# The last three sums of a seven-product pair split as one piece of 1536 columns

## The chip, the cores and the metric

The kernel runs on one core of one Trainium2 chip. The metric is the device time of one execution in microseconds; three runs of the kernel before gave 1866.25, 1866.78 and 1867.99 us, median 1866.78 us.

## The reference

One layer for 256 tokens of width 2048: a gated feed-forward block, a mixer, a second feed-forward block, each with an RMS norm ahead and a residual sum behind, and a last norm.

```python
x = x + 0.5 * swiglu(rmsnorm(x, ffn1_norm), w_gate, w_up, w_down)   # D_FF = 5632
h = rmsnorm(x, mix_norm); proj = h @ w_in                            # q, k, v of two mixers, gates, indexer
# retention over chunks of 128 tokens, sparse attention with the 64 best keys per query, rope on q and k
x = x + concat([ro, ao]) @ w_out
x = x + 0.5 * swiglu(rmsnorm(x, ffn2_norm), w_gate2, w_up2, w_down2)
return rmsnorm(x, final_norm)
```

Everything is in float32. Most of the arithmetic is in the six large products of the feed-forward blocks.

## The kernel before

**Precision.** A weight of 32 bits is split into two numbers of the matmul's format: `hi`, a rounded copy that ScalarE makes, and `lo = raw - hi`, that VectorE makes. A product of blocks is three matmuls (left hi by hi, left hi by lo, left lo by hi). So each weight that arrives by DMA passes once through ScalarE and once through VectorE before TensorE can use it.

**Pairs.** The wide products (gate and up, down, output) go by `wide` (L179). Two 128-row slices of the weights with 1024 columns, a pair, are one load of 128 x 2048 elements in a tile `raw` (ring of three). A pair of kind "C" takes the eight plain block products, 24 matmuls of 512 columns, from two pieces of 1024 columns. A pair of kind "S" is one step of a scheme with seven products, 21 matmuls, and needs sums of weight blocks: VectorE forms four of them in place (`less`, L278), three in piece 1 and one in piece 2. A pair of seven has four pieces: columns 512 to 1536, 1024 to 2048, 0 to 1024, and 1536 to 2048 alone.

**Chunks.** A chunk is 512 columns of gate and 512 of up with all eight pairs of K. The first chunk of each feed-forward block is plain; the other ten take the pairs in `ORDER` (L30): S C S C S C C C. A block runs six chunks, then `down` for these (two halves d = 0, 1 of 12 pairs, four of them S), then five chunks, then `down` (two halves of 10 pairs, four S). In all there are 95 S pairs: 60 in chunks, 32 in the down halves, 3 in the output product.

**Order.** The order on every engine is the program's own (`manual_schedule`). The main loop (L1089) walks the pieces: at step i it first runs `run_step(i)`, all work that was hung on that step, then `split(i + 4)`, then the matmuls of piece i. So a piece is split four pieces ahead, and `hi` and `lo` are rings of five tiles (`BUFS`, L39): the split of a piece waits until TensorE has finished the piece five before it. Work hung on steps: `sums_of` (L479) after the last S pair of a chunk, `ups` (L542) one piece before a chunk's end, `hidden` (L550) at its end (silu on ScalarE, products on VectorE), transposes of the result into M1 and M6 (`turn`, L563) and their split (`left_pair`, L332) in the next chunk.

**Other places.** `tables` (L650) computes sine and cosine tables on VectorE in steps, from the start of the first down stretch; `yield n` lets n pieces pass. Ahead of the input projection `turn_early` (L592) transposes four column pairs of x into the banks M1, M5, M6, M7, and `turn_late` the other four; `split_x` (L300) reads each bank by turns with ScalarE and VectorE. `rstd` and `row_of` (L439) make the row of norm factors by a small matmul of `diag`. The projection's chunks accumulate in bank pairs (`pair`, L93), the first in M5 and M6, the second in M1 and M7. `ret_mix` (L993) normalises and splits the retention's heads; the fourth call uses bank M8. In the plain first chunk, x itself is prepared pair by pair as it arrives (`first_x`, L397); for the three pairs that later chunks take as S, also the sums of its blocks (`s_of_x`, L362), in the order `FIRST` (L32).

Of the kernel before, what the change touches and what calls it, by code (L numbers as in the profile page):

```python
# [28 lines left out]
UP = "CSCSCSCC"  # L29
ORDER = (1, 0, 3, 2, 5, 4, 6, 7)  # L30
PLAIN = "CCCCCCCC"
FIRST = (0, 2, 4, 6, 7, 1, 3, 5)  # L32
DOWN = ("SCSCSCSCCCCC", "SCSCSCSCCC")
NH = 8
NI = 16
# [16 lines left out]
def layer(ctx: ExitStack, tc: tile.TileContext, a: dict, out: bass.AP):  # L52
# [103 lines left out]
    def mm_rows(chunk, n, kts, rhs, first, last):  # L156
# [21 lines left out]

    def wide(src, plan, left, x0=False, tail=False, order=None, sums=SUM):  # L179

        start = len(pieces)
        seen, last = {}, {}
        ending = [[], []]
        s_end = None

        def mm(i, off, a, m, at=None, p=None):

            for n, (u, v) in enumerate(((0, 0), (0, 1), (1, 0))):
                st = m not in seen
                seen[m] = 1  # L190
                e = [i, off, (pieces[i]["pair"], a), m, u, v, st, False]
                last[m] = e
                pieces[i if at is None else at]["mms"].append(e)

        for at, p in enumerate(order or range(len(plan))):
            kind = plan[p]
            loads.append([(0, block(src, 2 * at, 2 * at + 2, 1024))])
            if x0:
                loads[-1] = [lambda p=p: load_xT(p)] + [(o, loads[-1][0][1][:, o:o + n]) for o, n in
                                                        ([(0, 512), (512, 512), (1024, 1024)] if at == 0 else [(0, 2048)])]  # L200
            i = len(pieces)
            if kind == "C":
                tiles = [(0, 1024), (1024, 1024)]
                if x0 and at == 0:
                    tiles = [(0, 512), (512, 512), (1024, 1024)]
            else:
                tiles = [(512, 1024), (1024, 1024), (0, 1024), (1536, 512)]
            for k, (off, n) in enumerate(tiles):
                pieces.append(dict(load=len(loads) - 1, off=off, n=n, mms=[], left=left, pair=p,
                                   sums=k if kind == "S" else None, x=[p] if x0 and k == 0 else []))  # L210
            if kind == "C":
                for c in (1, 0):
                    for k in range(2):
                        off = 1024 * (1 - c) + 512 * k
                        j = max(j for j, (o, n) in enumerate(tiles) if o <= off)
                        for t in range(2):
                            if tail and p >= len(plan) - 2:
                                ending[t].append((i + j, off - tiles[j][0], p, (t, k), sums[f"{t + 1}{c + 1}"]))
                                continue
                            mm(i + j, off - tiles[j][0], (t, k), sums[f"{t + 1}{c + 1}"])  # L220
            else:
                for k, off, a, m in S_BLOCKS:
                    mm(i + k, off, a, m)
                s_end = len(pieces)

        ending[1].sort(key=lambda e: e[4], reverse=True)
        for t in range(2):
            for i, off, p, a, m in ending[t]:
                mm(i, off, a, m, i if t == 0 else len(pieces) - 1)
        for e in last.values():  # L230
            e[7] = True
        return start, s_end, len(pieces) - 1, len(pieces)
# [35 lines left out]
    def split(i):  # L268
        p = pieces[i]
        while n_loaded[0] < min(len(loads), p["load"] + 3):  # L270
            load(n_loaded[0])
            n_loaded[0] += 1
        for c in p.get("x", []):
            first_x(c, xT.pop(c))
        r = raws[p["load"]]
        raw = r[:, p["off"]:p["off"] + p["n"]]

        def less(a, b, o):  # L278
            V.tensor_tensor(r[:, o:o + 512], r[:, a:a + 512], r[:, b:b + 512], op=OP.subtract)  # L279


        k = p.get("sums")
        if k == 1:
            less(0, 1024, 1024)
        hi = new(wts, [P, 1024], F32R, "hi", BUFS)
        lo = new(wts, [P, 1024], F32R, "lo", BUFS)
        S.activation(hi[:, :p["n"]], raw, AF.Copy)  # L287
        if k == 1:
            less(0, 512, 0)
            less(512, 1024, 512)  # L290
        elif k == 2:
            less(1536, 512, 1536)
        V.tensor_tensor(lo[:, :p["n"]], raw, hi[:, :p["n"]].bitcast(F32), op=OP.subtract)  # L293
        split_of[i] = (hi, lo)

# [143 lines left out]
    def row_of(tok):  # L439

        diag = new(tmp, [P, 2, P], F32, "diag", 1)
        for t in range(2):
            V.tensor_scalar(diag[:, t], ident, tok[:, t:t + 1], None, op0=OP.mult)
        ps = small()
        yield 2
        for t in range(2):
            TE.matmul(ps[:, t * P:(t + 1) * P], lhsT=ones, rhs=diag[:, t], start=True, stop=True)
        return ps[:, :T]
# [142 lines left out]

    def turn_early(s_end, norm):  # L592

        for i, m in enumerate(("M1", "M5", "M6", "M7")):
            after(s_end + 2 + i, lambda i=i, m=m: turn_x(i, norm, m))

    def turn_late(end, norm, banks, later=0):

# [48 lines left out]

    rot_dram = new(dram, [P, 4, T], F32, "rot_dram")

    def tables():  # L650
        for k in range(2):
            ang, n = half_k("b"), half_k("sq")
            pi, pf = n[:, 0].bitcast(I32), n[:, 1]
            G.dma_start(pi, bass.AP(tensor=a["pos"].tensor, offset=a["pos"].offset, ap=[[0, P], [1, T]]))
            yield 4
            V.tensor_copy(pf, pi)
            for j in range(2):
                V.tensor_scalar(ang[:, j], pf, inv[:, k:k + 1], None, op0=OP.mult)
            yield 2
            V.tensor_scalar(n, ang, 1.0 / C_TWO_PI, None, op0=OP.mult)  # L660
            V.tensor_scalar(n[:, 0], n[:, 0], 0.25, None, op0=OP.add)
            yield 2
            V.tensor_scalar(n, n, MAGIC, None, op0=OP.add)
            V.tensor_scalar(n, n, MAGIC, None, op0=OP.subtract)
            for c in (C1, C2, C3):
                yield 2
                V.scalar_tensor_tensor(ang, n, -c, ang, op0=OP.mult, op1=OP.add)
            yield 1
            V.tensor_scalar(ang[:, 0], ang[:, 0], math.pi / 2, None, op0=OP.add)
            yield 1  # L670

            V.tensor_scalar(n, ang, 1.0 / C_TWO_PI, MAGIC, op0=OP.mult, op1=OP.add)
            V.tensor_scalar(n, n, MAGIC, None, op0=OP.subtract)
            for c in (C1, C2, C3):
                yield 2
                V.scalar_tensor_tensor(ang, n, -c, ang, op0=OP.mult, op1=OP.add)
            yield 2
            V.tensor_scalar(ang, ang, PI_DOWN, -PI_DOWN, op0=OP.min, op1=OP.max)
            yield 2
            S.activation(ang, ang, AF.Sin)  # L680
            yield 2
            V.tensor_scalar(ang[:, 1], ang[:, 1], sgn[:, k:k + 1], None, op0=OP.mult)
            G.dma_start(rot_dram[:, 2 * k:2 * k + 2], ang)
        yield 1
        act_table(AF.Silu)

# [14 lines left out]

    after(FIRST_SQ, first_squares)
    end = ffn(1, 0, 1, False)
    after(marks[1, 0, "down"] + 1, tables)
    after(marks[1, 1, "down"] + 4, load_tables)


# [6 lines left out]
        yield 2  # L714
        V.tensor_tensor(rot[:, :2], rot[:, :2], two(r_of[1]), op=OP.mult)

    after(m0 + 3, scaled_tables)

    heads = {}
    done_at = {}  # L720
# [26 lines left out]
    def cols(name, src, nchunks, idx=False, first=False):  # L747
# [7 lines left out]
        for c in range(nchunks):  # L755
            chunk = chunks[c]
            end = ends_[c] if c in ends_ else stream(src[c], kts, 256, 8, 4, rhs_x, chunk, mm_cols, 2)

            def done(chunk=chunk, c=c):
                if c % 2 == 0:  # L760
                    heads[name].append(big(shape=(P, 4, T)))
                return rope(chunk, 2, heads[name][c // 2][:, 2 * (c % 2):2 * (c % 2) + 2], idx,
                            3 if len(heads) == 1 and c == 0 else 1)

            after(end, done)
        done_at[name] = len(pieces)
# [42 lines left out]
    for c in range(4):  # L809
        chunk = Chunk()  # L810
        end = stream(a["w_rg"][c], list(range(KT)), 256, 8, 4, rhs_x, chunk, mm_cols, 2)

        def rg_done(chunk=chunk, c=c):
            b, g = evac(chunk, 2)
            V.tensor_tensor(g, g, two(r_of[1]), op=OP.mult)
            yield 1
            s = half_k("s")
            S.activation(s, g, AF.Silu)
            gate[c] = s

        after(end, rg_done)
        rg_end.append(end)
# [213 lines left out]
    after(s + 6, ret_norm)  # L1036
    for n in range(2):
        after(s + 7 + n, lambda n=n: ret_scale(n))
    for c in range(4):
        after(max(rg_end[c] + 2, s + 10 + 2 * c), lambda c=c: ret_mix(c))  # L1040

    class MixIn:
# [129 lines left out]
```

## Time and profile before

| | us |
|---|---|
| median of three runs | 1866.78 |
| profiled execution | 1868.15 |
| its span, first to last instruction | 1866.3 |
| TensorE busy | 1836.9 |
| VectorE busy | 1646.2 |
| ScalarE busy | 1072.9 |

The profiled execution is 1.4 us (0.07%) above the median. Busy time is the union of an engine's instructions; a busy TensorE is not TensorE at its peak, as its matmuls overlap. The mean granted TensorE clock is 0.997 of full speed. Idle time in front of an instruction is put down to the instruction of another engine that came last among those it waited for.

### The profile page before, as it was taken

Reading aid. Unit: us, or ns where it says so; the run is one execution under the profiler, and the core shown is the slowest. Engines: PE = TensorE matmul, PEld = TensorE weight load, DVE = VectorE, ACT = ScalarE, POOL = GpSimd, SP = SyncE. Lnnn points to the kernel's source line nnn. Section 1 sums busy time; section 2 is a strip of 40 time slices with the busy share of each in tenths; the row PEclk is TensorE's granted clock in tenths of the full one; section 3 lists DMA queues with packets and bytes.
Section 4 is the critical chain, followed back from the end, with each engine's and each line's share of the span. In section 5 each row is a group of like instructions: output and inputs, shape, how many; then the busy total and the mean of one; then the engine's idle time right before and its main releaser. Section 6 shows DMA issues by size and latency. Waiting matters only on the chain.

```text
span 1866.3 us, 22800 instructions
## 1 busy us (share of the span) xinstructions
PE 1836.9 (98%) x8643; PEld 1523.8 (82%) x8643; DVE 1646.2 (88%) x2122; ACT 1072.9 (57%) x1353; POOL 6.9 (0%) x17
## 2 busy tenths in 40 slices
PE   9999999999999999999999999999999999999997
PEld 7788787888888887988888888888888888888886
DVE  6999999999999997689865886799999889999997
ACT  7655655545565555656554566556555455555564
POOL 0000000000000000000000000000000000000000
PEclk9999999999999999999999999999999999999999
DMA  8545555565554544545434464555555555555454
GB/s 316 203 181 183 203 203 191 180 229 198 205 206 183 212 181 173 184 159 210 179 137 172 145 225 150 207 185 191 210 207 183 202 203 198 186 188 212 186 190 170
DMA packets 52237, 360.51 MB, mean 193 GB/s; under 512 B 5984, under 2 KB 5984, under 8 KB 9632
## 3 DMA queue, kind: packets, MB, share of 16 engines
q1 hardware_dynamic: 50976, 355.62, 51.6%
q0 software_dynamic: 576, 1.84, 0.3%
q10 hardware_dynamic: 576, 1.60, 0.3%
q8 instruction: 67, 1.10, 0.2%
q14 instruction: 42, 0.34, 0.1%
HBM read 356.42 MB, written 2.62 MB: 192 GB/s over the span
## 4 chain that ended last, share of the span: by engine, by line
PE 80%; DVE 12%; ACT 4%; issue 2%; DMA 2%; SPq 0%; ACTq 0%; DVEq 0%
PE M L236 63%; PE M L150 8%; DVE lo L293 7%; PE M L152 4%; DVE raw L279 2%; ACT hi L287 2%; PE M L168 1%; PE M L169 1%; PE M L167 1%; PE M L567 1%; DMA raw<-in_wgu 1%; DMA e<-in_xT 1%; DVE x L474 1%; ACT sq L416 0%; DVE e L477 0%
## 5 line engine op out<-in xcount | busy, mean ns | idle before, releaser
L287 ACT ACTIVATE hi<-raw 128x1024 fp32r<-128x1024 f32 (+2 forms) x859 | 844.6, 1006 | 561.5 <-DVE raw L279 359.5
L293 DVE TENSOR_TENSOR lo<-raw,hi 128x1024 fp32r<-128x1024 f32 (+2 forms) x859 | 976.4, 1159 | 122.1 <-ACT hi L287 108.7
L236 PE MATMUL M<-hi,xg 128*128 128x512 f32 x2240 | 725.5, 390 | 1.7 <-ACT e L546 1.5
L236 PE MATMUL M<-hi,mid 128*128 128x512 f32 x1690 | 527.4, 391 | 1.9 <-DVE e L1001 1.6
L236 PEld LDWEIGHTS M<-hi,xg 128*128 128x128 f32 x2240 | 420.5, 188 | 89.2 <-ACT e L546 1.9
L236 PE MATMUL M<-lo,xg 128*128 128x512 f32 x1120 | 437.9, 391 | 5.7 <-DVE lo L293 5.6
L236 PEld LDWEIGHTS M<-hi,mid 128*128 128x128 f32 x1690 | 317.2, 188 | 70.2 <-DVE e L1001 2.0
L236 PE MATMUL M<-lo,mid 128*128 128x512 f32 x845 | 329.8, 390 | 1.0 <-DVE lo L293 0.8
L279 DVE TENSOR_TENSOR raw<-raw 128x512 f32<-128x512 f32 x380 | 262.9, 692 | 12.7
L236 PEld LDWEIGHTS M<-lo,xg 128*128 128x128 f32 x1120 | 210.3, 188 | 55.5 <-DVE lo L293 12.7
L150 PE MATMUL M<-xg,hi 128*128 128x512 f32 x688 | 245.6, 401 | 0.4 <-DVE xg L307 0.3
L236 PEld LDWEIGHTS M<-lo,mid 128*128 128x128 f32 x845 | 158.6, 188 | 36.5 <-DVE lo L293 4.3
L152 PE MATMUL M<-xg,lo 128*128 128x256 f32 x645 | 180.9, 280 | 0.0
L150 PEld LDWEIGHTS M<-xg,hi 128*128 128x128 f32 x688 | 128.7, 189 | 30.3 <-issue 1.3
L236 PE MATMUL M<-hi,ext 128*128 128x512 f32 x360 | 141.2, 392 | 1.5 <-ACT s L557 1.4
L152 PEld LDWEIGHTS M<-xg,lo 128*128 128x128 f32 x645 | 122.3, 190 | 0.8
L236 PEld LDWEIGHTS M<-hi,ext 128*128 128x128 f32 x360 | 67.5, 188 | 18.9 <-DVE s L477 3.6
L236 PE MATMUL M<-lo,ext 128*128 128x512 f32 x180 | 70.1, 389 | 0.0
L477 DVE TENSOR_TENSOR s<-s,M 128x512 f32<-128x512 f32 x98 | 65.6, 683 | 1.9 <-PE M L236 0.9
L557 ACT ACTIVATE s<-s,r_tok 128x512 f32<-128x512 f32 x40 | 27.0, 718 | 53.5 <-DVE s L477 53.5
L477 DVE TENSOR_TENSOR e<-s,M 128x512 f32<-128x512 f32 x58 | 39.7, 684 | 1.0
L742 ACT ACTIVATE b<-e 64x512 f32<-64x512 f32 (+2 forms) x46 | 28.1, 612 | 19.8 <-DVE e L728 19.3
(176 smaller groups left out, 933.2 us busy)
## 6 DMA issues: line engine op xcount, KB each, us to landing
raw<-in_wgu SPq DMA_DIRECT2D x175, 1024.0 KB, 4.8
raw<-in_wd SPq DMA_DIRECT2D x88, 1024.0 KB, 4.8
raw<-in_w_out SPq DMA_DIRECT2D x16, 1024.0 KB, 4.9
raw<-in_w_iq SPq DMA_DIRECT2D x8, 1024.0 KB, 4.8
raw<-in_w_aq SPq DMA_DIRECT2D x8, 1024.0 KB, 4.7
raw<-in_w_rk SPq DMA_DIRECT2D x8, 1024.0 KB, 4.8
raw<-in_w_rq SPq DMA_DIRECT2D x8, 1024.0 KB, 4.7
raw<-in_w_rv SPq DMA_DIRECT2D x8, 1024.0 KB, 4.9
```

The source lines that it names most:

```text
L150: TE.matmul(acc, lhsT=hi[:, c:c + P], rhs=r, start=st, stop=sp)
L152: TE.matmul(acc[:, T:], lhsT=lo[:, c:c + P], rhs=r[:, :T], start=False, stop=False)
L167: TE.matmul(o, lhsT=h, rhs=hi[:, i * n:(i + 1) * n], start=st, stop=False)
L168: TE.matmul(o, lhsT=h, rhs=lo[:, i * n:(i + 1) * n], start=False, stop=False)
L169: TE.matmul(o, lhsT=l, rhs=hi[:, i * n:(i + 1) * n], start=False, stop=sp)
L236: TE.matmul(bank[m], lhsT=p["left"](pair, a)[u], rhs=split_of[i][v][:, off:off + 512], start=st, stop=sp)
L279: V.tensor_tensor(r[:, o:o + 512], r[:, a:a + 512], r[:, b:b + 512], op=OP.subtract)
L287: S.activation(hi[:, :p["n"]], raw, AF.Copy)
L293: V.tensor_tensor(lo[:, :p["n"]], raw, hi[:, :p["n"]].bitcast(F32), op=OP.subtract)
L477: V.tensor_tensor(o, a, b, op=OP.add)
L557: S.activation(u[b], bank[SUM[b]] if plain else u[b], AF.Silu, scale=r_tok[norm][:, t:t + 1])
L742: S.activation(b[p0:p0 + w], q[p1:p1 + w], AF.Copy)
```

## The change

A pair of seven gets a third piece of 1536 columns, blocks 0 to 1024 and the last sum, which is now written to columns 1024 to 1536; the fourth piece splits nothing and uses the third's tiles. These tiles, `hi3` and `lo3`, are of 1536 columns and have one buffer each, outside the rings. VectorE's `less` for the last sum now comes ahead of both copies by ScalarE, and one `lo` of 1536 columns follows. The room comes from the scratch for dynamic DMA, now 4096 bytes. Beside that, work hung on steps is moved: the order `FIRST`, the steps of `tables` and the start of the second table, `turn_early` (one step later, M5 last), `scaled_tables` and the small matmul in `row_of` (one step later each), the first two `rope`s, and the last `ret_mix` (right behind its gate).

```diff
-FIRST = (0, 2, 4, 6, 7, 1, 3, 5)
+FIRST = (0, 2, 1, 4, 3, 6, 5, 7)
...
-        (3, 0, "A22", "M4"))
+        (3, 1024, "A22", "M4"))
...
-                tiles = [(512, 1024), (1024, 1024), (0, 1024), (1536, 512)]
+                tiles = [(512, 1024), (1024, 1024), (0, 1536), (0, 1536)]
...
         k = p.get("sums")
+        if k == 3:
+            split_of[i] = split_of[i - 1]
+            return
+        n, ring = (1536, "3") if k == 2 else (1024, "")
         if k == 1:
             less(0, 1024, 1024)
-        hi = new(wts, [P, 1024], F32R, "hi", BUFS)
-        lo = new(wts, [P, 1024], F32R, "lo", BUFS)
-        S.activation(hi[:, :p["n"]], raw, AF.Copy)
+        hi = new(wts, [P, n], F32R, "hi" + ring, 1 if ring else BUFS)
+        lo = new(wts, [P, n], F32R, "lo" + ring, 1 if ring else BUFS)
         if k == 1:
+            S.activation(hi, raw, AF.Copy)
             less(0, 512, 0)
             less(512, 1024, 512)
         elif k == 2:
-            less(1536, 512, 1536)
+            less(1536, 512, 1024)
+            for o in (0, 512):
+                S.activation(hi[:, 2 * o:2 * o + 1024 - o], raw[:, 2 * o:2 * o + 1024 - o], AF.Copy)
+        else:
+            S.activation(hi[:, :p["n"]], raw, AF.Copy)
         V.tensor_tensor(lo[:, :p["n"]], raw, hi[:, :p["n"]].bitcast(F32), op=OP.subtract)
...
-        yield 2
+        yield 3
         for t in range(2):
             TE.matmul(ps[:, t * P:(t + 1) * P], lhsT=ones, rhs=diag[:, t], start=True, stop=True)
...
-        for i, m in enumerate(("M1", "M5", "M6", "M7")):
-            after(s_end + 2 + i, lambda i=i, m=m: turn_x(i, norm, m))
+        for i, m in enumerate(("M1", "M6", "M7", "M5")):
+            after(s_end + 3 + i, lambda i=i, m=m: turn_x(i, norm, m))
...
-    def tables():
+    def tables(second):
...
+            if k == 0:
+                yield second - now[0]
...
-    after(marks[1, 0, "down"] + 1, tables)
+    after(marks[1, 0, "down"] + 1, lambda: tables(marks[1, 0, "down"] + 31))
...
-    after(m0 + 3, scaled_tables)
+    after(m0 + 4, scaled_tables)
...
-                            3 if len(heads) == 1 and c == 0 else 1)
+                            (5, 4)[c] if len(heads) == 1 and c < 2 else 1)
...
             gate[c] = s
+            if c == 3:
+                ret_mix(c)
...
-    for c in range(4):
+    for c in range(3):
         after(max(rg_end[c] + 2, s + 10 + 2 * c), lambda c=c: ret_mix(c))
...
-    nc = bacc.Bacc("TRN2", target_bir_lowering=False, num_devices=1)
+    nc = bacc.Bacc("TRN2", target_bir_lowering=False, num_devices=1, dynamic_dma_scratch_size=4096)
```

In `tables`, every yield of 4 becomes 3, every 2 between two of VectorE's instructions becomes 1, and instructions that stood together are parted by a yield of 1: 22 steps for a table in place of 28.

## Rows read from the trace of the kernel before

**Rows 1.** The page: busy time by engine; shares of the chain that ended last.
```profile
PE 1836.9 (98%) x8643; PEld 1523.8 (82%) x8643; DVE 1646.2 (88%) x2122; ACT 1072.9 (57%) x1353; POOL 6.9 (0%) x17
...
PE 80%; DVE 12%; ACT 4%; issue 2%; DMA 2%; SPq 0%; ACTq 0%; DVEq 0%
```

**Rows 2.** Windows of four chunks: stretch, length, busy by engine, clock, DMA, GB/s.
```profile
52.23:98.05 45.82, 43.00 (x193) 35.02 (x192) 43.28 (x52) 29.31 (x35) 0.00 (x0) 1.00 0.53 197
98.05:141.12 43.07, 42.73 (x193) 35.02 (x191) 41.34 (x52) 25.19 (x29) 0.00 (x0) 1.00 0.52 196
...
1195.26:1237.63 42.37, 42.37 (x192) 35.18 (x191) 39.25 (x47) 25.45 (x29) 0.00 (x0) 1.00 0.54 199
...
1577.95:1620.34 42.39, 42.39 (x193) 35.17 (x192) 40.07 (x49) 25.51 (x29) 0.00 (x0) 1.00 0.55 199
```

**Rows 3.** VectorE's groups in the chunk at 98.05: busy, mean ns, idle before.
```profile
L293 DVE TENSOR_TENSOR lo<-raw,hi 128x1024 fp32r<-128x1024 f32 x19 | 22.8, 1221 | 0.9 <-ACT hi L287 0.5
L279 DVE TENSOR_TENSOR raw<-raw 128x512 f32<-128x512 f32 x12 | 8.3, 692 | 0.4
```

**Rows 4.** VectorE's timeline, one wait in the same chunk: start, us, instruction, idle.
```profile
126.88 1.22 DVE L293 TENSOR_TENSOR lo<-raw,hi 128x1024 fp32r<-128x1024 f32 x1 [0.55 <-ACT hi L287]
```

**Rows 5.** VectorE's timeline over pieces 1 to 3 of one S pair.
```profile
105.82 2.14 DVE L279 TENSOR_TENSOR raw<-raw 128x512 f32<-128x512 f32 x3
107.88 1.22 DVE L293 TENSOR_TENSOR lo<-raw,hi 128x1024 fp32r<-128x1024 f32 x1
109.13 0.69 DVE L279 TENSOR_TENSOR raw<-raw 128x512 f32<-128x512 f32 x1
109.74 1.82 DVE L293 TENSOR_TENSOR lo<-raw,hi 128x1024 fp32r<-128x1024 f32 x2
```

**Rows 6.** ScalarE's timeline, the copy of the same pair's fourth piece.
```profile
109.94 2.53 ACT L287 ACTIVATE hi<-raw 128x512 fp32r<-128x512 f32 x3 [0.80 <-DVE raw L279]
```

**Rows 7.** Groups by shape, whole span, of the pieces of 512 columns.
```profile
L293 DVE TENSOR_TENSOR lo<-raw,hi 128x512 fp32r<-128x512 f32 x97 | 66.4, 685 | 2.8 <-ACT hi L287 2.8
...
L287 ACT ACTIVATE hi<-raw 128x512 fp32r<-128x512 f32 x97 | 61.4, 633 | 81.4 <-DVE raw L279 66.4 <-PE M L236 13.9 <-DMA raw<-in_wgu 1.2
```

**Rows 8.** Windows of four down halves; the first two hold the tables.
```profile
270.67:337.10 66.43, 64.28 (x285) 52.39 (x284) 62.86 (x83) 34.35 (x38) 1.08 (x2) 1.00 0.55 197
337.10:400.36 63.26, 63.17 (x278) 51.64 (x276) 60.40 (x79) 32.13 (x35) 0.55 (x1) 1.00 0.56 204
613.52:667.04 53.52, 53.20 (x238) 43.46 (x236) 51.16 (x60) 30.07 (x34) 0.00 (x0) 1.00 0.55 206
...
1410.44:1473.91 63.47, 63.47 (x286) 52.63 (x284) 56.80 (x65) 34.55 (x37) 0.00 (x0) 1.00 0.55 200
```

**Rows 9.** TensorE's waits: line, waited for, us in total, times, longest.
```profile
PE M L236 <- DVE lo L293: 6.4, 19, 0.7
PE M L447 <- DVE diag L443: 2.4, 1, 2.4
PE M L567 <- DVE s L477: 2.0, 1, 2.0
PE M L236 <- DVE e L1001: 1.6, 1, 1.6
PE M L236 <- ACT e L546: 1.5, 1, 1.5
...
PE M L236 <- ACT s L557: 1.4, 1, 1.4
```

**Rows 10.** Timelines of TensorE, VectorE, ScalarE: a bank of x transposed, one split.
```profile
713.32 0.66 PE L405 MATMUL M<-ident,x 128*128 128x128 f32 x4 [1.38 <-DVE e L477]
...
710.75 0.48 DVE L307 SCALAR_TENSOR_TENSOR xg<-M,gains,xg 128x256 fp32r<-128x256 f32 x1 [0.54 <-ACT xg L306]
...
710.24 0.47 ACT L306 ACTIVATE xg<-M,gains 128x256 fp32r<-128x256 f32 x1 [0.55 <-DVE xg L307]
```

**Rows 11.** Window behind the wait for `diag`, columns as in group 2.
```profile
742.10:745.60 3.50, 3.44 (x12) 3.06 (x13) 3.50 (x6) 2.05 (x3) 0.00 (x0) 0.52 0.28 87
```

More of the change, by code (lines that the diff above doesn't have):

```diff
@@ L654, in tables @@
             G.dma_start(pi, bass.AP(tensor=a["pos"].tensor, offset=a["pos"].offset, ap=[[0, P], [1, T]]))
-            yield 4
+            yield 3
             V.tensor_copy(pf, pi)
@@ L658, in tables @@
                 V.tensor_scalar(ang[:, j], pf, inv[:, k:k + 1], None, op0=OP.mult)
-            yield 2
+            yield 1
             V.tensor_scalar(n, ang, 1.0 / C_TWO_PI, None, op0=OP.mult)
+            yield 1
             V.tensor_scalar(n[:, 0], n[:, 0], 0.25, None, op0=OP.add)
-            yield 2
+            yield 1
             V.tensor_scalar(n, n, MAGIC, None, op0=OP.add)
+            yield 1
             V.tensor_scalar(n, n, MAGIC, None, op0=OP.subtract)
             for c in (C1, C2, C3):
-                yield 2
+                yield 1
                 V.scalar_tensor_tensor(ang, n, -c, ang, op0=OP.mult, op1=OP.add)
@@ L672, in tables @@
             V.tensor_scalar(n, ang, 1.0 / C_TWO_PI, MAGIC, op0=OP.mult, op1=OP.add)
+            yield 1
             V.tensor_scalar(n, n, MAGIC, None, op0=OP.subtract)
             for c in (C1, C2, C3):
-                yield 2
+                yield 1
                 V.scalar_tensor_tensor(ang, n, -c, ang, op0=OP.mult, op1=OP.add)
-            yield 2
+            yield 1
             V.tensor_scalar(ang, ang, PI_DOWN, -PI_DOWN, op0=OP.min, op1=OP.max)
@@ L1038, in layer @@
         after(s + 7 + n, lambda n=n: ret_scale(n))
-    for c in range(4):
+    assert rg_end[3] + 1 >= s + 16
+    for c in range(3):
         after(max(rg_end[c] + 2, s + 10 + 2 * c), lambda c=c: ret_mix(c))
```

## The prediction

> **What bounds the kernel now.** I read first the busy times and the chain that ended last: TensorE is busy 98% of the span and holds 80% of the chain, VectorE holds 12% [rows 1]. A share over the whole span hides stages, so next come the windows of single chunks [rows 2]. A chunk in which nothing makes TensorE wait lasts 42.4 us (the one at 1195.26, the one at 1577.95); inside these there is still some 0.3 us of small delays, so TensorE's own need is about 42.1 us. The chunk at 98.05 lasts 43.07 us, with VectorE busy for 41.34 of them. Fourteen of the twenty chunks that hold S pairs look like this one; the other six, the first behind each plain chunk and the first two behind each down stretch, are shorter or, at 52.23, longer. The reader is to see that VectorE is 96% busy in such a chunk, and that its idle 1.73 us are not spare: the groups [rows 3] put 0.9 of them ahead of `lo`, of which only some 0.6 are waits for a free ring slot (0.55 in one place, [rows 4]); 0.4 stand ahead of `less`, 34 ns each for the result of the instruction before; and the rest is VectorE waiting for a copy or a silu of ScalarE that its own last result released. So VectorE needs 41.4 + 1.1 = 42.5 us for a chunk that TensorE could do in 42.1. In these chunks VectorE is the bound, by a little. TensorE's waits say the same: 19 waits for `lo` [rows 9], about one per chunk, at the first C pair of the new chunk.
>
> **The merged piece.** Removed is one instruction per S pair: `lo` of 1024 and `lo` of 512 become one of 1536. The pair of them takes 1.82 us from first start to last end [rows 5], with 0.685 for the second [rows 7], so the 1024 columns occupy 1.14 us before the next may start, and the 512 about 0.61. 512 columns more cost 0.53, which leaves 0.08 us of fixed cost: that is what a merge saves, and 1536 columns should take 1.67 where the two took 1.75.
>
> [...]
>
> Added is a wait. Now `less` for the last sum ends, and VectorE goes straight on to `lo` of piece 2, whose copy is long made; meanwhile ScalarE copies the 512 new columns, and that copy is hidden behind the 1.14 us of `lo` [rows 5, 6]. After the change the one `lo` needs that copy too, and nothing stands between `less` and `lo` in VectorE's queue, since both are inside one `split`. `less` starts at 109.13, the copy at 109.94, and it takes 0.633 [rows 5 to 7], so it ends at 110.57; VectorE could have started at 109.74. The wait is 0.83 us, with the step back to VectorE about 0.85. Bounds: not below 0.63 (the copy alone), not above 1.5 (that and the copy of 1024 columns behind it in ScalarE's queue, were it late). Behind it in VectorE's queue stand all later splits and evacuations. Net per S pair: 0.85 - 0.08 = +0.77 us of VectorE's queue; three pairs in a chunk, +2.3.
>
> The tiles of their own give something back: fewer pieces turn in the ring, so the 0.6 us of waits for slots go (I count them all as gone). `hi3` with one buffer costs nothing: its next use comes six pieces later and its split four ahead, so it waits for the piece just finished, as the ring did.
>
> **A chunk after.** 41.4 + 2.3 + 1.1 = 44.8 us against 43.1: +1.7, VectorE-bound, TensorE waiting some 2.5 us per chunk. Ten chunks have no lead from a slack stretch: +17.0. After a plain chunk or a down stretch VectorE has about 2 us of lead; I let it absorb the first chunk (0), most of the second (+0.3 twice behind a down stretch, +0.5 twice behind a plain one), and a part of the third behind a down stretch (+1.1 twice): +3.8.
>
> **Down halves.** With four S pairs VectorE needs 3.1 us more per half. The long half at 1410.44 has 63.47 of length and 56.80 of VectorE [rows 8], so only the debt of the chunk before it shows at its start: +2.0; its second half 0. The short halves (53.52, VectorE 51.16) become VectorE-bound like a chunk: +1.7 each for d = 0, +0.6 each for d = 1, twice: +4.6. The two halves with the tables carry some 6.1 us more of VectorE (62.86 against 56.80), now packed into the first 23 steps, where S pairs stand and where VectorE has no slack left. At least the half cannot be shorter than VectorE's need, 62.86 + 3.1 + 1.5 of unavoidable idle = 67.4 (+1.0); at most all of the table and the debt show (+5.5); I take +3.5 and, for the second table by the same reckoning from 60.40, +2.5.
>
> **Moved steps.** `FIRST` spreads the x sums over the plain chunk. The waits for ScalarE's `e` and `s` (1.5 and 1.4, [rows 9]) go, and the chunk at 52.23 becomes like the one at 1195.26: 45.82 - 42.37 = -3.4. Later `turn_early` frees the wait for `e` L477, -1.4 [rows 10]. But M5, now transposed last, is transposed at the first step of the projection, and M5 is where that first step accumulates: TensorE must wait until `ready` (two products of 512 columns, 0.61 us each as worked out above) and then ScalarE and VectorE by turns, some 0.5 us each, four times, have read the bank, less 0.7 us of its own transposes [rows 10]: +2.5, bounds 0 and 4.3 (with a clock loss as below). [...] Sum -3.0. The last `ret_mix` moves ahead of the wait for `e` L1001: -1.6, against three S pairs in the output product: +1.7; together 0. The 4 KB scratch and its few transfers on POOL, busy 6.9 us in all [rows 1]: between 0 and 2 us, off TensorE's path; I take 0. The `rope` steps shift work within the projection, where no `rope` stands among TensorE's waits [rows 9]: between -0.5 and 1, I take 0.
>
> **Sum.** 17.0 + 3.8 + 2.0 + 4.6 + 6.0 - 3.4 - 3.0 + 0 = +27.0 on the profiled 1868.15, which is 1.4 above the median of the runs: 1895.2 there, 1894 as a median.
>
> **Rivals.** *The free slots decide.* If ScalarE's copy were hidden after all (wait under 0.25 us, the point at which the chunk falls below 43.1), VectorE's need would fall to about 42.3, and fourteen chunks gain 0.8: -11; with -3.4, -4.1 - 1.4, -1.6 and some 2 in the table halves it ends near 1844. For it: the ring's waits are in the trace [rows 4], and the merge does shorten VectorE's queue. Against it: the copy needs `less`, and `lo` needs the copy, in a queue that is served in order. Chance 0.12. *The clock falls too.* If the new waits, at fourteen places 1.7 us or more, each sent TensorE to the lower level as the 2.4 us at 742 did, each would cost up to 1.7 more: +24, 1918. Against it: the wait of 2.0 us for `s` [rows 9] left the clock of its stretch at 1.00 [rows 8], and a TensorE that waits for VectorE anyway loses little. Chance 0.05. *Both sides cancel:* gains at the moved steps as above, the wait half hidden, no table cost: 1867. Chance 0.04.
>
> **How the numbers follow.** The forecast has 0.79. Its own ends: ScalarE's answers overlap better (chunk 44.2), no table cost and no wait for M5 give 1879; the tables in full, a clock loss at M5 and all old idle kept give 1908. Drawn a little wider, 1874 to 1910, it leaves out the faster rival and most of the clock's. About 0.2%, 3.7 us, is what a measurement of this kernel can tell from no change: faster 0.12, same 0.04, slower 0.84.
>
> **What would show it.** In the changed trace `lo` of 1536 columns should stand about 95 times, 1.75 us each, with some 0.85 us idle before each, put down to `hi`: about 80 us in all. The steady chunks should last near 44.8 us with VectorE without other gaps, and TensorE's waits for `lo` should grow from 6.4 to over 30 us. The waits for `diag`, `e` L546 and `s` L557 should be gone, and a new one of some 2.5 us should stand at the first matmul of the projection. I am wrong if the idle time before the long `lo` is short, or if chunks stay at 43 us with it.

## The result, and the profile after

The changed kernel takes 1912.66 us (median of four runs, 1911.50 to 1914.03) against 1867.38 for the kernel before beside it: a ratio of 1.0241, 95% interval 1.0229 to 1.0254, or +45.3 us. It is slower, as forecast, by the mechanism that was forecast, but by 18 us more than the sum said, and 2.7 us above the upper end of the range, 1910. The profiled execution took 1913.43 us, its span 1911.6.

The page of the changed kernel, busy times and the chain that ended last:

```profile
PE 1847.1 (97%) x8643; PEld 1523.0 (80%) x8643; DVE 1633.0 (85%) x2027; ACT 1058.7 (55%) x1353; POOL 6.9 (0%) x17
...
PE 42%; DVE 37%; ACT 11%; DMA 5%; issue 4%; ACTq 0%; SPq 0%; DVEq 0%
```

VectorE does less work than before, 13 us and 95 instructions less [rows 1], and yet its share of the chain went from 12% to 37%: an engine's share of the chain can grow because it waits, and not only because it works.

VectorE's groups by shape, whole span (busy us, mean ns | idle before, put down to):

```profile
L301 DVE TENSOR_TENSOR lo<-raw,hi 128x1024 fp32r<-128x1024 f32 x661 | 786.4, 1220 | 114.1 <-ACT hi L300 108.6
...
L301 DVE TENSOR_TENSOR lo<-raw,hi 128x1536 fp32r<-128x1536 f32 x95 | 167.1, 1759 | 66.4 <-ACT hi L298 66.4
```

The long `lo` stands 95 times with 1.76 us each, and 66.4 / 95 = 0.70 us of idle before each, all put down to the copy. VectorE's timeline over one such piece, and ScalarE's line for the copy of its last 512 columns:

```profile
153.79 1.22 DVE L301 TENSOR_TENSOR lo<-raw,hi 128x1024 fp32r<-128x1024 f32 x1
155.05 0.69 DVE L279 TENSOR_TENSOR raw<-raw 128x512 f32<-128x512 f32 x1
156.44 2.89 DVE L301 TENSOR_TENSOR lo<-raw,hi 128x1536 fp32r<-128x1536 f32 x2 [0.70 <-ACT hi L298]
```

```profile
155.78 0.63 ACT L298 ACTIVATE hi<-raw 128x512 fp32r<-128x512 f32 x1 [0.72 <-DVE raw L279]
```

Read it as a round trip: `less` starts at 155.05, the copy can start at 155.78, and `lo` at 156.44, 1.39 us after `less`. Before, the next `lo` began 0.61 us after `less` [rows 5]. So 0.78 us per pair went into the trip, where the prediction had 0.85; less the 0.08 that the merge saves, 0.70 against 0.77.

Windows of the changed kernel: two chunks (the one behind the plain first chunk, a steady one), the two halves with the tables, a short half, the chunk behind the second block's plain one, a long half (stretch, length, busy by engine, clock, DMA share, GB/s):

```profile
52.59:97.20 44.61, 43.31 (x193) 34.95 (x191) 38.90 (x45) 27.57 (x33) 0.00 (x0) 1.00 0.51 189
...
142.48:187.63 45.15, 43.31 (x193) 34.94 (x192) 41.10 (x49) 24.77 (x29) 0.54 (x1) 1.00 0.52 189
278.05:348.70 70.65, 64.94 (x286) 52.15 (x284) 63.90 (x81) 36.22 (x40) 1.08 (x2) 1.00 0.53 187
348.70:414.91 66.21, 63.49 (x277) 51.57 (x276) 59.95 (x75) 32.01 (x35) 0.54 (x1) 1.00 0.53 195
634.15:689.53 55.38, 53.51 (x237) 43.39 (x236) 50.80 (x56) 29.27 (x33) 0.00 (x0) 1.00 0.54 199
...
1222.56:1264.94 42.38, 42.38 (x193) 35.18 (x191) 38.07 (x44) 24.43 (x29) 0.00 (x0) 1.00 0.51 195
1445.10:1509.61 64.51, 64.09 (x285) 52.47 (x284) 57.23 (x63) 35.54 (x39) 0.00 (x0) 1.00 0.53 197
```

The steady chunk went from 43.19 us (141.12 to 184.31 before; 43.07 for its neighbour in [rows 2]) to 45.15 us, although VectorE is busy a little less in it, 41.10 against 41.49 us; the chunk at 1222.56 has the same splits and loses nothing, because it starts with a lead. TensorE's waits (line, waited for, us in total, times, longest):

```profile
PE M L236 <- DVE e L485: 21.9, 16, 1.6
PE M L236 <- DVE lo L301: 18.5, 43, 1.9
PE M L150 <- DVE xg L315: 6.2, 1, 6.2
```

The 40 us of the first two lines are VectorE's lateness as TensorE meets it: 18.5 us at a split, and 21.9 at `e`, the evacuation of a bank that stands behind the long `lo` in VectorE's queue. The third line is the start of the projection. The waits for `diag` and for `e` L1001 of [rows 9] are gone. The prediction wanted over 30 us in the waits for `lo` alone; there are 18.5, and more than half of the lateness shows at `e`.

Stage by stage, from windows cut at the same matmuls in both traces:

| stage | forecast | measured |
|---|---|---|
| ten steady chunks | +17.0 | +20.2 (1.7 to 2.3 each) |
| chunks with a lead | +3.8 | +7.4 (2.2, 1.3, 1.9, 1.9; five others 0) |
| halves with the tables | +6.0 | +7.2 (4.2, 3.0) |
| other down halves, without the last of the first block | +6.0 | +6.2 |
| plain chunk and the one behind it | -3.4 | -0.9 (+0.3, -1.2) |
| last half of the first block, projection | -2.4 | +3.4 |
| first chunk of the output product | 0 | +1.4 |
| ahead of the first and behind the last matmul of the wide products | 0 | +0.4 |
| sum | +27.0 | +45.3 |

### The profile page after: what moved, and what is told of

It is laid out like the page before. It is cut to its first block, busy times and chain, and to the rows that moved or that the text cites. A ratio compares the mean times of both kernels' runs of the same rounds, so it can differ in the third digit from the quotient of the medians.

```text
span 1911.6 us, 22558 instructions
## 1 busy us (share of the span) xinstructions
PE 1847.1 (97%) x8643; PEld 1523.0 (80%) x8643; DVE 1633.0 (85%) x2027; ACT 1058.7 (55%) x1353; POOL 6.9 (0%) x17
## 4 chain that ended last, share of the span: by engine, by line
PE 42%; DVE 37%; ACT 11%; DMA 5%; issue 4%; ACTq 0%; SPq 0%; DVEq 0%
PE M L236 25%; DVE lo L301 20%; DVE raw L279 10%; PE M L150 8%; ACT hi L300 7%; DMA raw<-in_wgu 4%; PE M L152 4%; DVE e L485 2%; ACT hi L298 2%; DVE s L485 1%; DMA raw<-in_wd 1%; PE M L168 1%; PE M L169 1%; PE M L167 1%; DVE x L482 1%
## 5 line engine op out<-in xcount | busy, mean ns | idle before, releaser
L301 DVE TENSOR_TENSOR lo<-raw,hi 128x1024 fp32r<-128x1024 f32 (+2 forms) x764 | 955.3, 1283 | 182.5 <-ACT hi L300 110.6
L300 ACT ACTIVATE hi<-raw 128x1024 fp32r<-128x1024 f32 (+1 forms) x574 | 576.5, 1046 | 187.9 <-PE M L236 70.9
L292 ACT ACTIVATE hi<-raw 128x1024 fp32r<-128x1024 f32 x95 | 101.0, 1063 | 309.9 <-DVE raw L279 307.5
L150 PE MATMUL M<-xg,hi 128*128 128x512 f32 x688 | 246.5, 402 | 6.2 <-DVE xg L315 6.2
L298 ACT ACTIVATE hi<-raw 128x1024 fp32r<-128x1024 f32 (+1 forms) x190 | 161.0, 847 | 107.6 <-DVE raw L279 106.9
L152 PE MATMUL M<-xg,lo 128*128 128x256 f32 x645 | 181.5, 281 | 0.0
L150 PEld LDWEIGHTS M<-xg,hi 128*128 128x128 f32 x688 | 129.3, 189 | 36.0 <-DVE xg L315 6.4
L152 PEld LDWEIGHTS M<-xg,lo 128*128 128x128 f32 x645 | 122.9, 190 | 0.7
```

The lines of the kernel that those rows point to most:

```text
L150: TE.matmul(acc, lhsT=hi[:, c:c + P], rhs=r, start=st, stop=sp)
L152: TE.matmul(acc[:, T:], lhsT=lo[:, c:c + P], rhs=r[:, :T], start=False, stop=False)
L292: S.activation(hi, raw, AF.Copy)
L298: S.activation(hi[:, 2 * o:2 * o + 1024 - o], raw[:, 2 * o:2 * o + 1024 - o], AF.Copy)
```

## The experiments

All differ from the changed kernel or from the one before by a few lines; the kernel before ran beside each, at 1867.3 to 1867.6 us.

**The moved steps alone**, with the old split:

```diff
 # against the changed kernel: tiles of pieces, split() and hi/lo rings as before
-                tiles = [(512, 1024), (1024, 1024), (0, 1536), (0, 1536)]
+                tiles = [(512, 1024), (1024, 1024), (0, 1024), (1536, 512)]
```

> The changed kernel with the split of before (two pieces of 1024 and 512 columns in the rings of five); all moved steps and the small scratch stay. Theory (the copy of the last sum, laid bare, makes the loss): steady chunks are back at 43.1 us, so this kernel lies within 6 us of before: gains at the first S chunk (about -3), at diag (-4.1) and at the last ret_mix (-1.6), against the wait for M5 with its half clock (+8 as the changed kernel's trace shows, less 1.4), together near 1867. Rival (the moved steps make the loss): above 1895, and the split alone near before.

Measured: 1867.79 us, ratio 1.000 (0.9991 to 1.0010). TensorE's longest wait, and a window around the entry to the projection:

```profile
PE M L150 <- DVE xg L307: 5.6, 1, 5.6
```

```profile
717.00:731.00 14.00, 8.36 (x41) 7.00 (x40) 8.31 (x12) 4.72 (x8) 0.00 (x0) 0.88 0.41 150
```

The moved steps with the 4 KB scratch cost nothing together, and none of the 45 us. But this zero is a balance: the `diag` wait is gone, and a wait of 5.6 us at the projection, with the clock down behind it (0.88 over the window shown, 0.51 from 726.0 to 729.4 us), has come.

**The split alone**, all steps where they were:

```diff
 # against the kernel before: the new split (a part of it is shown), the tiles of pieces 3 and 4, the scratch
+        n, ring = (1536, "3") if k == 2 else (1024, "")
...
+            less(1536, 512, 1024)
+            for o in (0, 512):
+                S.activation(hi[:, 2 * o:2 * o + 1024 - o], raw[:, 2 * o:2 * o + 1024 - o], AF.Copy)
```

> The kernel before with the new split, its tiles and the small scratch alone; no step is moved. Theory: 95 waits of 0.70 us ahead of the lo of 1536 columns, steady chunks near 45.2 us, no wait for M5, the waits for diag and at the first S chunk still there: 1905 to 1914. Rival (moved steps): 1862 to 1872.

Measured: 1911.46 us, ratio 1.0233 (1.0218 to 1.0248), +43.8. A steady chunk, the window behind the wait for `diag`, and TensorE's waits:

```profile
145.04:190.16 45.12, 43.31 (x193) 34.95 (x191) 41.10 (x49) 24.77 (x29) 0.54 (x1) 1.00 0.52 190
...
764.00:772.00 8.00, 5.59 (x34) 4.78 (x33) 7.36 (x16) 5.60 (x9) 0.00 (x0) 1.00 0.40 132
```

```profile
PE M L236 <- DVE e L485: 21.8, 16, 1.7
PE M L236 <- DVE lo L301: 15.8, 42, 1.5
...
PE M L236 <- ACT e L554: 2.8, 1, 2.8
PE M L455 <- DVE diag L451: 2.4, 1, 2.4
```

The split carries all the loss: +43.8 and +0.2 from the run above leave 1.3 of the 45.3 us for the two together. The waits of 2.4 us for `diag` and of 2.8 us for `e` are as long as those of the kernel before or longer, and yet the clock was 1.00 in the window shown, and its mean over the traced execution was 0.998, where the kernel before had 0.997.

**Is it the wait, or the tiles?** The tiles, both copies and their order stay; only the long `lo` becomes two instructions, so that 1024 columns can go while the last 512 are copied:

```diff
-        V.tensor_tensor(lo[:, :p["n"]], raw, hi[:, :p["n"]].bitcast(F32), op=OP.subtract)
+        if k == 2:
+            for a, b in ((0, 1024), (1024, 1536)):
+                V.tensor_tensor(lo[:, a:b], raw[:, a:b], hi[:, a:b].bitcast(F32), op=OP.subtract)
+        else:
+            V.tensor_tensor(lo[:, :p["n"]], raw, hi[:, :p["n"]].bitcast(F32), op=OP.subtract)
```

> The changed kernel with one edit: lo of the 1536-column piece is made by two instructions, of 1024 and then 512 columns, in the same tiles. The copy of the last sum is then hidden behind the first of them. Theory: the idle time ahead of lo falls from 66 us in all to under 5, VectorE gains 95 times 0.62 (0.70 less 0.08 for one instruction more), steady chunks fall to 42.5 to 43.4, and the kernel to 1865 to 1877 (the wait for M5 stays). Rival (tiles with a single buffer hold ScalarE and VectorE back): the time stays above 1900.

Measured: 1867.83 us, ratio 1.0003 (0.9994 to 1.0012). VectorE's groups, and a steady chunk:

```profile
L303 DVE TENSOR_TENSOR lo<-raw,hi 128x1024 fp32r<-128x1024 f32 x95 | 115.8, 1219 | 0.0
...
L303 DVE TENSOR_TENSOR lo<-raw,hi 128x512 fp32r<-128x512 f32 x95 | 65.1, 685 | 0.0
```

```profile
527.09:570.19 43.10, 42.93 (x192) 35.04 (x191) 41.19 (x52) 24.89 (x29) 0.00 (x0) 1.00 0.51 195
```

The idle time goes from 66.4 us to 0.0 and the whole loss with it, with two tiles, scratch and moved steps in place. A wait of 0.70 us, 95 times, in a queue where everything behind it waits too, was the loss. The tiles of their own give nothing back: 43.10 us is the old chunk.

**The size of the wait.** The two copies change places, so that ScalarE makes the 512 columns first and the other 1024 behind them:

```diff
-            for o in (0, 512):
+            for o in (512, 0):
```

> The changed kernel with its two copies by ScalarE for the 1536 columns in the other order: the 512 new columns first, then the 1024. The copy of 1024 columns, until now made behind the lo of piece 1, is then laid bare too: the idle time ahead of the long lo grows from 0.70 to some 1.65 us, 90 us over 95 pairs. Theory (a laid-bare copy costs its length wherever VectorE is the bound): steady chunks near 48 us, the whole 1955 to 1985. Rival (VectorE has slack that takes up such waits, and the changed kernel's loss has another source): below 1925.

Measured: 2000.59 us, ratio 1.0716 (1.0700 to 1.0732), 16 above the expected band. The long `lo`, and two steady chunks:

```profile
L301 DVE TENSOR_TENSOR lo<-raw,hi 128x1536 fp32r<-128x1536 f32 x95 | 167.0, 1758 | 161.8 <-ACT hi L298 161.8
```

```profile
147.61:195.78 48.17, 45.01 (x193) 36.07 (x191) 41.18 (x48) 24.45 (x30) 0.54 (x1) 0.96 0.49 178
524.70:572.92 48.22, 43.73 (x193) 34.86 (x192) 41.17 (x48) 24.49 (x31) 0.00 (x0) 1.00 0.46 175
```

The idle time before `lo` grew by 1.00 us (161.8 / 95 = 1.70 against 0.70), and a chunk with three S pairs by 3.0 us: the price is one to one. The steady chunks are where the expectation had them; it was low on the chunks that had a lead, which lose it (the second chunk behind a down stretch, 42.39 us before and after the change, takes 46.05 here). The clock now falls too, to 0.96 in the first of these chunks; its mean over the traced execution is 0.981, against 0.996 for the changed kernel. But the second chunk, at 1.00, takes as long as the first, 48.22 us against 48.17: in these chunks, where TensorE waits for VectorE anyway, the lower clock cost nothing that shows.

**Why do the own tiles give nothing?** In the run with two `lo` a chunk still holds a wait for the weights' DMA (ScalarE, then VectorE):

```profile
554.65 1.06 ACT L300 ACTIVATE hi<-raw 128x1024 fp32r<-128x1024 f32 x1 [1.66 <-DMA raw<-in_wgu]
...
555.75 1.23 DVE L305 TENSOR_TENSOR lo<-raw,hi 128x1024 fp32r<-128x1024 f32 x1 [0.81 <-ACT hi L300]
```

Each wide load was cut into two transfers of 1024 columns, so that a piece need not wait for the other's half:

```diff
-            loads.append([(0, block(src, 2 * at, 2 * at + 2, 1024))])
+            b = block(src, 2 * at, 2 * at + 2, 1024)
+            loads.append([(0, b)] if x0 else [(0, b[:, :1024]), (1024, b[:, 1024:])])
```

> The kernel with two lo's for the 1536 columns (e3_two_lo), and each wide load of 2048 columns in two transfers of 1024, so that a C pair's first piece can be copied when half has landed. Theory on the tiles of their own (the ring's waits went, but VectorE then runs ahead into the weights' transfer: 0.81 us in each steady chunk): ScalarE's waits for transfers of the wide weights fall from 47 us to under 20, steady chunks from 43.1 to 42.3 to 42.7, the whole to 1855 to 1862. Rival (the chunk is bound by VectorE's own work, and any wait taken away comes back elsewhere): within 2 us of e3_two_lo, 1867.8.

Measured: 1867.57 us, ratio 0.9999 (0.9990 to 1.0008): the theory missed, the rival held. ScalarE's waits for the loads of the feed-forward weights fell from 47.2 to 28.6 us. The chunk, and the same place on VectorE:

```profile
527.30:570.40 43.10, 42.93 (x193) 35.06 (x192) 41.23 (x52) 24.89 (x29) 0.00 (x0) 1.00 0.57 195
```

```profile
555.70 1.23 DVE L306 TENSOR_TENSOR lo<-raw,hi 128x1024 fp32r<-128x1024 f32 x1 [0.21 <-ACT hi L301]
...
557.48 0.29 DVE L335 TENSOR_TENSOR sq<-b 128x128 f32<-128x128 f32 x1 [0.56 <-ACT b L350]
```

The 0.81 us became 0.21 + 0.56: VectorE now waits for a copy of TensorE's transposes. The wait moved from ring slot to DMA to transposes, and the chunk stayed at 43.10 us. Which dependency holds the 43.1 us these runs don't settle.

**The entry to the projection.** The changed kernel with the old `turn_early` (one step earlier, M5 second):

```diff
-        for i, m in enumerate(("M1", "M6", "M7", "M5")):
-            after(s_end + 3 + i, lambda i=i, m=m: turn_x(i, norm, m))
+        for i, m in enumerate(("M1", "M5", "M6", "M7")):
+            after(s_end + 2 + i, lambda i=i, m=m: turn_x(i, norm, m))
```

> The changed kernel with the order and the steps of turn_early as before (M1, M5, M6, M7 from the second step on). Theory: the wait of 6.2 us at the first matmul of the projection and the 6.8 us at half clock behind it go, the wait for e ahead of the transposes returns (1.4 or more, VectorE being later): 5 to 8 us less than the changed kernel. Rival (VectorE's queue is late there anyway, whatever the bank): within 2 us of it.

Measured: 1907.16 us (1.0211, 1.0195 to 1.0226), 5.5 less than the changed kernel. The wait of 6.2 us is gone from TensorE's list, and this one of [rows 10] is back:

```profile
PE M L413 <- DVE e L485: 1.4, 1, 1.4
```

**A version that beats both.** The old split, `FIRST` and the other moved steps as changed, but `turn_early` and `tables` as before (in `tables` the yields of 4 and 2, no `second`):

```diff
 # against the kernel before; beside these, scaled_tables, the ropes, the loop over the other ret_mix and the scratch as changed
-FIRST = (0, 2, 4, 6, 7, 1, 3, 5)
+FIRST = (0, 2, 1, 4, 3, 6, 5, 7)
...
-        yield 2
+        yield 3
...
+            if c == 3:
+                ret_mix(c)
```

> The moved steps alone with the old split (e1_moved_only), and with turn_early and the steps of tables as before; what is left of the change is FIRST, row_of, scaled_tables, the first two ropes and the last ret_mix. Theory (these remove waits of TensorE, and only the bank M5 and the packed tables took the gain away): 1867.8 less 5.6 for M5 less 1.5 for the tables, 1858 to 1863, faster than before by 0.25 to 0.5%. Rival (what they free is lost again further on): within 2 us of before.

Measured: 1860.93 us, ratio 0.9967 (0.9955 to 0.9978), 6.5 us better than the kernel before. TensorE's waits, and a window that begins 1.2 us behind the wait for `s`:

```profile
PE M L236 <- DVE lo L293: 7.4, 22, 0.8
PE M L567 <- DVE s L477: 2.0, 1, 2.0
PE M L405 <- DVE e L477: 1.4, 1, 1.4
```

```profile
311.26:314.67 3.41, 3.41 (x9) 2.63 (x8) 3.41 (x6) 1.05 (x2) 0.00 (x0) 0.50 0.64 269
```

Three neighbours follow. First, two `lo` and halved loads in place of the old split, with `turn_early` and `tables` as before:

```diff
 # against the kernel with halved loads
-        for i, m in enumerate(("M1", "M6", "M7", "M5")):
+        for i, m in enumerate(("M1", "M5", "M6", "M7")):
-            after(s_end + 3 + i, lambda i=i, m=m: turn_x(i, norm, m))
+            after(s_end + 2 + i, lambda i=i, m=m: turn_x(i, norm, m))
...
-    after(marks[1, 0, "down"] + 1, lambda: tables(marks[1, 0, "down"] + 31))
+    after(marks[1, 0, "down"] + 1, tables)
```

> e5_half_loads with turn_early and the steps of tables as before: own tiles, two lo's, half transfers, and the moved steps that gain. Theory: the gains add up, 1847 to 1856. Rival (half transfers bring nothing): 1859 to 1863, as the one without the tiles.

Measured: 1861.38 us, ratio 0.9970 (0.9960 to 0.9979): the same time, so own tiles and halved loads give nothing here either, and the rival held.

With the banks turned in the order M1, M6, M5, M7, at the old steps:

```diff
-        for i, m in enumerate(("M1", "M5", "M6", "M7")):
+        for i, m in enumerate(("M1", "M6", "M5", "M7")):
```

> The mended moved steps (e7_moved_mended) with the banks of turn_early in the order M1, M6, M5, M7 at the old steps: M5, read last by the sums, is transposed one step later than before, and M7, which the projection needs two pieces after M5, stays last. Theory (each bank's wait is set by who reads it last and who writes it first): the wait of 1.4 us for e ahead of the transposes goes and none comes at the projection's start: 1858.5 to 1860.5, 1 to 2 us under e7_moved_mended. Rival (the transposes wait for VectorE's queue, not for a bank): equal to it within 0.7 us.

Measured: 1861.28 us, ratio 0.9968 (0.9957 to 0.9980): no gain, as the rival said. TensorE's waits show the trade, 1.4 us for `e` against 1.1 and 0.3:

```profile
PE M L150 <- DVE xg L307: 1.1, 1, 1.1
...
PE M L405 <- DVE x L474: 0.3, 1, 0.3
```

With the old order `FIRST`:

```diff
-FIRST = (0, 2, 1, 4, 3, 6, 5, 7)
+FIRST = (0, 2, 4, 6, 7, 1, 3, 5)
```

> The mended moved steps (e7_moved_mended) with FIRST as before, the S pairs of x last. It prices the new order by itself. By the prediction's term the first S chunk takes 3.4 us longer without it (45.8 against 42.4); by the chunks' windows of the runs so far (45.8 against 43.3 there, and the plain chunk 0.7 longer with the new order) it is 1.5 to 2.5 us: 1862.5 to 1863.5 for the whole. Rival (start and first chunk cancel): within 0.7 us of e7_moved_mended.

Measured: 1863.59 us, ratio 0.9979 (0.9970 to 0.9988), 0.1 above the expected band. The medians put `FIRST` at 2.3 to 2.7 us (against 1861.28 and 1860.93); the intervals overlap, so the size is rough.

## Why the prediction's mechanism was right and its sum was not

**What failed.** The direction and the mechanism were right, but terms of the sum were too small. Three of them make 12.6 of the 18.3 us that were missing: the wait for M5 at the projection (+5.8 with the half before it), the lead that was to absorb debt (+3.6), and the waits for slots that were counted as gone (+3.2). `FIRST` gave 2.5 less than forecast, the output product took 1.4 more, and the rest is 1.8.

**The mechanism: right, and shown.** The wait ahead of the long `lo` is there 95 times, put down to the copy; taking it away alone took the loss away, and lengthening it by 1.00 us lengthened a chunk by 3.0. Its size was nearly right: 0.78 us by starts against 0.85, and 0.70 against 0.77 net of the merge, so 2.1 in a chunk of three pairs where the forecast had 2.3. The merged instruction occupies 2.89 - 1.22 = 1.67 us of the queue, as worked out. It lasts 1.759 us by itself. The 1.75 us that the prediction expected of it is an estimate that 0.685 us for 512 columns [rows 7] and 1.221 for 1024 [rows 3] give, with as much again for the next 512 (1.757); the queue pays the 1.67.

**The steady chunk: 44.8 forecast, 45.2 measured (+3.2 over ten).** The step that failed is "so the 0.6 us of waits for slots go (I count them all as gone)". A chunk paid 2.0 us, all but the whole 2.1 of the three pairs, so next to nothing came back. The waits for slots did shrink. ScalarE's waits before the change and after it:

```profile
ACT hi L287 <- PE M L236: 126.5, 169, 2.5
...
ACT hi L287 <- DMA raw<-in_wgu: 11.3, 15, 1.8
```

```profile
ACT hi L300 <- PE M L236: 70.9, 52, 1.7
ACT hi L300 <- DMA raw<-in_wgu: 51.4, 23, 2.6
```

What TensorE's slots no longer held, the loads did: 40 us more of waiting for DMA. For VectorE, each steady chunk keeps a stall of 0.8 to 1.0 us, now behind a load, where it had 0.4 to 0.8 before:

```profile
127.78 1.06 ACT L300 ACTIVATE hi<-raw 128x1024 fp32r<-128x1024 f32 x1 [2.38 <-DMA raw<-in_wgu]
```

```profile
128.87 1.22 DVE L301 TENSOR_TENSOR lo<-raw,hi 128x1024 fp32r<-128x1024 f32 x1 [0.81 <-ACT hi L300]
```

The prediction asked of every stall that goes what is late next, but not of this one.

**The chunks with a lead (+3.6).** Behind a down stretch the lead was sized well: three chunks with some 2.0 us of debt each paid 1.9 in all, so 4.1 was absorbed, where the forecast absorbed 3.7; the rest is the larger debt per chunk. Behind the plain chunk of the second block it paid 1.3 in place of 0.5. The real miss is the first block: its second chunk behind the plain one paid 2.2 in full, because the chunk ahead of it already ended late.

**The entry to the projection: the largest miss (+5.8 with the half before it).** The forecast took +2.5 for M5, bounds 0 to 4.3. VectorE's timeline and TensorE's, around that wait:

```profile
744.42 1.28 DVE L482 SCALAR_TENSOR_TENSOR x<-M,x 128x512 f32<-128x512 f32 x2
745.62 0.47 DVE L315 SCALAR_TENSOR_TENSOR xg<-M,gains,xg 128x256 fp32r<-128x256 f32 x1
746.63 0.48 DVE L315 SCALAR_TENSOR_TENSOR xg<-M,gains,xg 128x256 fp32r<-128x256 f32 x1 [0.54 <-ACT xg L314]
747.58 1.23 DVE L301 TENSOR_TENSOR lo<-raw,hi 128x1024 fp32r<-128x1024 f32 x1 [0.46 <-ACT hi L300]
748.72 1.28 DVE L482 SCALAR_TENSOR_TENSOR x<-M,x 128x512 f32<-128x512 f32 x2
749.92 0.47 DVE L315 SCALAR_TENSOR_TENSOR xg<-M,gains,xg 128x256 fp32r<-128x256 f32 x1
750.93 0.48 DVE L315 SCALAR_TENSOR_TENSOR xg<-M,gains,xg 128x256 fp32r<-128x256 f32 x1 [0.54 <-ACT xg L314]
```

```profile
744.67 0.60 PE L413 MATMUL M<-ident,x 128*128 128x128 f32 x4
751.47 0.79 PE L150 MATMUL M<-xg,hi 128*128 128x512 f32 x1 [6.21 <-DVE xg L315]
```

M5 is transposed by 745.27, but its two reads by VectorE, at 749.92 and 750.93, stand behind everything issued before them: not the one pair of `x` sums that the prediction counted, but two pairs, the two reads of M7, and a `lo` that itself waits for ScalarE. What failed is the list of what is queued ahead of the reads. Then the clock:

```profile
750.08:756.90 6.82, 5.43 (x17) 4.66 (x18) 2.02 (x3) 1.42 (x2) 0.00 (x0) 0.50 0.37 144
```

In 6.8 us at 0.50 TensorE worked for 5.43. The pairs of L150 and L152 began 0.64 us apart there and 0.35 at a clock of 1.00 (from 1084.72 us on), so by an estimate some 2.5 of the 5.43 us were lost; the forecast had one drop worth 1.7 in its upper bound. The run that undid the move of `turn_early` prices it: in the two traces the stretch up to the first matmul of the projection differs by 4.7 us (the 6.2 less the wait of 1.4 for `e`), and the stretch from there on by 1.5 (334.6 us against 333.2), so what the lower clock cost came to little more than that. The medians differ by 5.5 us, where the terms -1.4 and +2.5 made +1.1. The rest of that stretch went as forecast: with the old `turn_early` it lasts 390.37 us against 393.19 before, of which `diag` gave about 4.4 (forecast 4.1), as the half ahead of it lost 1.6 at a wait for its last `x`. No run shows the -4.1 of the sum by itself: the trace of before has the wait of 2.4 us [rows 9] and 3.50 us at 0.52 behind it [rows 11], from which 1.7 us lost to the clock is an estimate (3.50 times 0.48; the bound of 4.3 and the rival on the clock use it too), and in place of the term the runs showed these 4.4 us as a difference of stretches. In the version that beats both the same stretch takes 389.10, 4.1 less than before. That includes the clock behind the wait, which is not certain to fall: in the run of the split alone the window behind the same wait of 2.4 us stands at 1.00.

**`FIRST`: -3.4 forecast, -1.2 there.** The waits for `e` and `s` shrank to 0.3 and 0.8 us rather than going, and this chunk has no lead, so the split's loss begins in it. With the old split the chunk was 43.27 us, 2.5 less than before, and in the last run above the order was worth 2.3 to 2.7: even alone it is less than the 3.4 of the sum, which compared it with a chunk that has a lead.

**Smaller terms.** The tables' halves cost +7.2 (forecast 6.0); the run of the split alone has +5.4 there and that of the moved steps +1.6, so most of it is the split and not the packed tables. The other halves cost 6.2 (6.0). In the output product the wait for `e` L1001 went, but two waits for `lo` of 1.8 us in all came, and the window's TensorE time went from 42.61 busy and 1.63 idle to 43.43 and 2.23: +1.4 in place of 0. The prediction put the S pairs at +1.7 there and let the wait that went pay for all of it. In the whole output product the split alone costs 2.0 us and the moved steps alone give 0.6, not 1.6. The scratch and `rope` at nothing: not tried alone, but together with the other moves they cost nothing that can be measured.

**The rivals.** "The free slots decide" fell: with the copy hidden (the two-`lo` run) the chunk is 43.10, not the 42.3 that it needs. "The clock falls too" gives 1918, close to the time measured, but for the wrong reason: in the steady chunks the clock is 1.00, and the new drop stands at the projection. "Both sides cancel" fell with the first: the wait is not half hidden, and the kernel is not near 1867.

## What to carry to other kernels

Merging two instructions of VectorE's queue made the first part wait for what only the second part needed, 0.70 us of idle time 95 times; price such a round trip (here 0.78 us) against the fixed cost saved (0.08), per occurrence. When a step is moved later, list every instruction then queued ahead of its reads on every engine, from the schedule rather than from the nearest neighbour. In this chain of closely matched engines a stall that went was replaced each time (slots by loads, loads by transposes), so count such a gain as nothing until the next late thing is named.

## What the runs showed of the hardware that was not expected

The way from VectorE to ScalarE and back costs little more than the work in the pair shown above at 155.05 us: from the start of `less` (0.69 us) to the copy's start 0.73 us, from the copy's start (0.63 us) to the start of `lo` 0.66.

What a wait does to the granted clock does not follow from its length here. In the changed kernel, from 1.4 us before the end of the wait of 6.2 us, it stood at 0.50 for 6.8 us, about twice the stretch behind the 2.4 us wait [rows 11]. At the same place a wait of 5.6 us came with a window of 3.4 us at 0.51 in the run of the moved steps, whose traced execution had a mean clock of 0.997; with a wait of 5.6 us there the run with two `lo` and the one with halved loads had a mean of 0.996. The wait of 2.0 us for `s` was followed by 3.4 us at 0.50 in the traced execution of the version that beats both (mean 0.997) and left the clock at 1.00 in the kernel before (306 to 318 us); the run with the banks in the order M1, M6, M5, M7, with the same wait, had a mean of 0.998. In the split alone, with waits of 2.4 and 2.8 us, the mean was 0.998. In the run with swapped copies, with twenty waits for `e` of up to 2.7 us, it was 0.981. Waits of up to 1.9 us in the changed kernel left the clock at 1.00 (278 to 415 us).
